# Attention's loads in a fixed order, results through other queues, and projections moved ahead of a diagonal

## The chip, the cores and the metric

The kernel runs on one core of one Trainium2 chip. The metric is the device time of one execution in microseconds (us). Shapes below are partitions x elements, and 2.4 and 1.2 GHz are the two levels of TensorE's clock.

## What is computed

One layer of a streaming encoder on 1024 tokens of width 1024, all in float32: a feed-forward network, a mixer of two head groups, a second feed-forward network, each with a residual and a layer norm. The change touches the mixer alone. Cut to that:

```python
def gla_chunked(q, k, v, log_a):       # 4 heads, dk 64, dv 128, chunks of 64 tokens
    def step(S, inp):
        A = jnp.einsum('bhid,bhjd,bhijd->bhij', qn, kn, jnp.exp(diff))
        o = jnp.einsum('bhij,bhjv->bhiv', A, vn) + jnp.einsum('bhid,bhdv->bhiv', qn * jnp.exp(b), S)
        ...
def dsa_attention(q, k, v, q_idx, k_idx, w_idx):   # 8 heads of 64, blocks of 128 queries
        _, idx = lax.top_k(score, topk)            # 256 keys of each query
        p = jax.nn.softmax(logits, axis=-1)        # over the selected keys
        return jnp.einsum('bqhk,bqkhd->bqhd', p.astype(vg.dtype), vg)

proj = h @ w_in
o_gla = (o.reshape(B, T, GLA_WIDTH) * jax.nn.silu(gg.astype(f32))).astype(h.dtype)
return jnp.concatenate([o_gla, o_dsa], axis=-1) @ w_out
```

## The kernel before

**Products.** A float32 product is made of three passes over a high and a low part (`whi`, `wlo` of the weights, `xh`, `xl` of the input), so one step of a projection is three matmuls (lines 655 to 657 with features on the partitions, tile `pf`; lines 672 to 674 with tokens on the partitions, tile `pt`), and a finished tile takes eight steps, 24 matmuls. Weights come as `raw` tiles of 512 KB (line 71, two buffers of a rotating pool); ACT makes `whi` (line 72), and POOL, in four pieces (line 75), or DVE (line 77) makes `wlo`.

**The stages.** After the first feed-forward network and the index scores come the search for the selected keys (line 785) and the masks (`keep_keys`, lines 820 to 829, on DVE, one call for each block of queries from the third on), which the scheduler spreads over the gated linear attention (GLA). GLA runs as two pairs of heads, `gla_pair(0)` and `gla_pair(1)`. A pair has two halves of 512 tokens. A half starts with a diagonal (line 974 on POOL makes the product `kz`, line 977 on PE sums it to `pd`, line 980 on DVE spreads it into the tile `at`); seven levels follow (POOL line 998, DVE line 999, PE line 1005 to `pa`, DVE line 1016 into `at`), then the products with values and states into `po` (lines 1033 and 1036) and the norm and gate: squares on ACT (line 1044), a root on POOL (line 207), the gate into `og` on DVE (line 1049), and a store to `og_dram` (line 1058). Pair 0 is done when pair 1 begins.

**What fills pair 1.** Pair 1 is a generator, `side`; the generator `fill` gives steps of other projections: first eight token tiles of the pair's own values and gates (`gvg`, lines 672 to 674), then `dq_steps`, eight tiles of attention's queries (lines 655 to 657), four for each half `i` of the tokens. A loop takes one part of `side` and then so many steps of `fill`; PE runs in the order in which this is written, the other engines in an order that a scheduler made. The tuple of counts in that loop has 8 times 8 + 7 times 8 = 120 steps in both kernels. A finished query tile goes through `stage_split`: ACT copies the high part (line 1404), DVE makes the low part (line 1405), and both are stored to DRAM, `q_hi` and `q_lo` (line 1407). Suffix numbers in the names: `q_hi_81` and `q_lo_82` are the first half of the queries, `q_hi_83` and `q_lo_84` the second; `k_hi_85` and `k_lo_86` are the first half of the keys, `k_hi_87` and `k_lo_88` the second.

**Attention** (`attend`) reads all that again in another layout. Keys go into `kst`, two tiles for even and odd heads, here named `xh` and `xl` (line 1545), values into `vt` (line 1546); a block's queries go into a pair `qq`, `ql` (lines 1072 and 1073), of which there are two, filled in turn by `load_q`. For each of eight blocks of 128 queries and each head there are logits (lines 1100 and 1101, tile `lg`), the mask and the maximum on DVE (line 1104), the exponential on ACT (line 1116), transposes (line 1127), and the product with values (line 1143). When a block starts, `begin` loads the GLA result of that block, `cat` (line 1555); `end` turns it (line 194) and, a block later, makes a part of the output projection (lines 672 to 674), for which the weights `raw` of `in_w_out` are wanted.

**Queues.** Every DMA of the kernel before is issued by SP, in one order. An instruction of SP that waits holds back all that stand behind it. A DMA also waits for the one eight places ahead of it, since completion is counted on eight semaphores in rotation.

Of the kernel before, what the change touches and what calls it, by code (L numbers as in the profile page):

```python
# [7 lines left out]
F32 = mybir.dt.float32  # L8
# [10 lines left out]
P = 128  # L19
# [6 lines left out]
HT = T // 2  # L26
# [89 lines left out]
class Block:  # L116
# [759 lines left out]
    def gla_pair(self, p, g, gp, go, sgp, ps, masks, consts, o_dram):  # L876

        nc = self.nc
# [77 lines left out]
        for i in range(2):  # L956
# [7 lines left out]
            for step, L in enumerate((0, 64, 32, 16, 8, 4, 2, 1)):  # L964
# [22 lines left out]
                n = HT // (2 * L)  # L987
# [51 lines left out]
            for h in range(2):  # L1039
# [8 lines left out]
                for j in range(4):  # L1048
# [8 lines left out]
                c0 = p * 256 + h * P  # L1057
                nc.sync.dma_start(
                    o_dram[i * HT : (i + 1) * HT, c0 : c0 + P].rearrange("(b t) f -> t b f", t=P), og
# [125 lines left out]
    def run(self):  # L1185
# [160 lines left out]
        with ExitStack() as s2:  # L1346
# [8 lines left out]
            with ExitStack() as s3:  # L1355
# [45 lines left out]

                def stage_split(pt, dst, t, i):
                    part = [sgp.tile([P, 512], F32R, tag=f"og{j}", name=self.uid("part")) for j in range(2)]
                    nc.scalar.activation(part[0], pt, AF.Copy)
                    nc.vector.tensor_sub(part[1], pt, part[0])
                    for j in range(2):
                        nc.sync.dma_start(dst[i][j][t * P : (t + 1) * P, :], part[j].bitcast(F32))

# [70 lines left out]
                def dq_steps():  # L1479
                    for i in range(2):  # L1480
                        for t, u in enumerate(um["dq"]):
                            for k, pt in enumerate(self.proj_steps(u, i, x1T)):
                                if i == 0 and t < 2 and k == 3:
                                    self.w.need(um["dq"][t + 2], um["dq"][t + 2], 1)
                                if k < KD - 1:
                                    yield
                            stage_split(pt, q_dram, t, i)
                            yield
# [18 lines left out]
                with self.in_order():  # L1507
                    for n in (14,) + (6,) * 7 + (8, 0, 0, 0) + (7,) * 8:
                        next(side)
                        for _ in range(n):  # L1510
                            next(fill)
                    for _ in side:
                        pass
# [17 lines left out]
            for i, pool in enumerate((q0, q1)):  # L1531
# [4 lines left out]
                qp.append((qq, ql))  # L1536
                self.load_q(i, q_dram, qp[i])
            vt = [p.tile([P, 4, 512], F32, name=f"vt{i}") for i, p in enumerate((vp0, vp))]
            def load_keys(i):
                cs = slice(i * HT, (i + 1) * HT)  # L1540
                for e in range(2):
                    for j in range(2):
                        r0 = 64 * (e ^ j)
                        src = k_dram[i][j].rearrange("(q e d) t -> e d q t", e=2, d=64)
                        nc.sync.dma_start(kst[e][r0 : r0 + 64, :, cs].bitcast(F32), src[e])
                nc.sync.dma_start(vt[i], dv_dram[i].rearrange("(b t) f -> t b f", t=P))

            load_keys(0)
            c0 = self.new_half(1)
            cat = []  # L1550
            with tc.tile_pool(name="ps_att", bufs=1, space=PSUM, reuse_waits="tile") as ps:
                def begin(b):
                    c = catp.tile([P, D], F32, tag="cat", name=self.uid("cat"))
                    cat.append(c)
                    nc.sync.dma_start(c[:, 0:512], og_dram[b * P : (b + 1) * P, :])
                    if b == 0:
                        self.w.need(um["out"][0], um["out"][0] + 3)
                    if b == 1:
                        load_keys(1)
                    return c  # L1560
# [11 lines left out]

                self.attend(kst, vt, bias, q_dram, qp, ep, tp, rp, ps, begin, end)

        with ExitStack() as st, ExitStack() as ff_stack:
# [112 lines left out]
```

## Time and profile before

| what | value |
|---|---|
| median of 3 runs | 2039.76 us (2038.33 to 2041.39) |
| the profiled execution | 2041.8 us, span 2040.0 us |
| busy share of the span | PE 96%, DVE 72%, ACT 40%, POOL 29% |
| mean granted TensorE clock | 0.983 |
| DMA | 298.43 MB, mean 146 GB/s over the span |
| pair 1 of GLA | about 985 to 1138 us |
| attention | about 1128 to 1305 us |

All times below are microseconds from the start of the span of the profiled execution. A wait is given with the instruction that waited on the left and the one that released it on the right. A matmul's own duration overlaps with the next one; what counts is the distance between two starts.

### The profile page before, as it was taken

Reading aid. Unit: us, or ns where it says so; the run is one execution under the profiler, and the core shown is the slowest. Engines: PE = TensorE matmul, PEld = TensorE weight load, DVE = VectorE, ACT = ScalarE, POOL = GpSimd, SP = SyncE. Lnnn points to the kernel's source line nnn. Section 1 sums busy time; section 2 is a strip of 40 time slices with the busy share of each in tenths; the row PEclk is TensorE's granted clock in tenths of the full one; section 3 lists DMA queues with packets and bytes.
Section 4 is the critical chain, followed back from the end, with each engine's and each line's share of the span. In section 5 each row is a group of like instructions: output and inputs, shape, how many; then the busy total and the mean of one; then the engine's idle time right before and its main releaser. Section 6 shows DMA issues by size and latency. Waiting matters only on the chain.

```text
span 2040.0 us, 26930 instructions
## 1 busy us (share of the span) xinstructions
PE 1958.7 (96%) x9752; PEld 1608.2 (79%) x9752; DVE 1475.2 (72%) x2330; ACT 823.8 (40%) x1321; POOL 587.6 (29%) x499
## 2 busy tenths in 40 slices
PE   8999999999999999999798699999999999999997
PEld 6888888888888788777576578787888888888886
DVE  5587788785668768899973366566687887876577
ACT  4332332324334345898432355333323323334341
POOL 3345445430001102144333000044454454420001
PEclk9999999999999999998899799999999999999999
DMA  5345445469656322022106631342354454478664
GB/s 175 114 143 188 145 154 179 142 224 320 195 179 200 103 83 84 20 63 73 31 27 177 187 91 37 104 155 82 126 181 145 150 177 149 155 274 273 204 193 151
DMA packets 192708, 298.43 MB, mean 146 GB/s; under 512 B 16304, under 2 KB 98368, under 8 KB 192576
## 3 DMA queue, kind: packets, MB, share of 16 engines
q1 hardware_dynamic: 192576, 296.72, 44.8%
q8 instruction: 76, 1.25, 0.3%
q14 instruction: 56, 0.46, 0.1%
HBM read 205.96 MB, written 90.70 MB: 145 GB/s over the span
## 4 chain that ended last, share of the span: by engine, by line
PE 75%; DVE 11%; DMA 5%; issue 3%; POOL 2%; ACT 2%; SPq 1%; POOLq 0%; DVEq 0%; ACTq 0%
PE pd L491 18%; PE pq L319 12%; PE pq L321 12%; PE pq L320 12%; DVE junk L785 3%; PE pf L655 2%; PE pf L656 2%; PE pf L657 2%; PE pv L1143 2%; PE tpe L1127 2%; PE pt L672 2%; PE pt L673 1%; PE pt L674 1%; PE tp L265 1%; DVE ee L991 1%
## 5 line engine op out<-in xcount | busy, mean ns | idle before, releaser
L97 DVE TENSOR_TENSOR wloq<-rw,whiq 128x512 fp32r<-128x512 f32 (+1 forms) x208 | 213.7, 1030 | 111.0 <-ACT whiq L96 110.2
L97 DVE TENSOR_TENSOR wlod<-rd,whid 128x1024 fp32r<-128x1024 f32 x154 | 186.4, 1220 | 129.0 <-ACT whid L96 128.0
L96 ACT ACTIVATE whid<-rd 128x1024 fp32r<-128x1024 f32 x154 | 160.9, 1059 | 244.4 <-PE pd L491 168.8
L96 ACT ACTIVATE whiq<-rw 128x512 fp32r<-128x512 f32 (+1 forms) x208 | 163.4, 806 | 225.0 <-POOL rw L305 94.0
L491 PE MATMUL pd<-wlod,whid 128*128 128x512 f32 x616 | 239.8, 390 | 0.9 <-DVE wlod L97 0.8
L491 PE MATMUL pd<-whid,wlod 128*128 128x512 f32 x616 | 239.3, 389 | 0.0
L491 PE MATMUL pd<-whid 128*128 128x512 f32 x616 | 235.0, 391 | 0.0
L319 PE MATMUL pq<-b_h,whiq 128*128 128x512 f32 x576 | 228.4, 397 | 2.0 <-ACT b_h L96 2.0
L320 PE MATMUL pq<-b_l,whiq 128*128 128x512 f32 x576 | 225.0, 391 | 1.2 <-DVE b_l L97 1.2
L321 PE MATMUL pq<-b_h,wloq 128*128 128x512 f32 x576 | 224.9, 391 | 0.0
L207 POOL TENSOR_TENSOR rs<-ve,neghalf 128x1 f32<-128x1 f32 x24 | 33.8, 1410 | 619.3 <-DVE ve L225 619.3
L431 ACT ACTIVATE c<-c 128x512 f32<-128x512 f32 x80 | 50.5, 632 | 237.4 <-DVE c L355 135.8
L319 PE MATMUL pq<-xh,whiq 128*128 128x512 f32 x352 | 137.7, 391 | 0.0
L321 PE MATMUL pq<-xh,wloq 128*128 128x512 f32 x352 | 137.0, 389 | 0.0
L320 PE MATMUL pq<-xl,whiq 128*128 128x512 f32 x352 | 136.9, 389 | 0.0
L491 PEld LDWEIGHTS pd<-wlod,whid 128*128 128x128 f32 x616 | 115.7, 188 | 25.5 <-DVE wlod L97 2.1
L491 PEld LDWEIGHTS pd<-whid 128*128 128x128 f32 x616 | 115.5, 188 | 24.7 <-ACT whid L96 1.0
L491 PEld LDWEIGHTS pd<-whid,wlod 128*128 128x128 f32 x616 | 115.6, 188 | 24.1
L672 PE MATMUL pt<-whi,xh 128*128 128x512 f32 x320 | 131.9, 412 | 2.4 <-ACT stage L1475 1.5
L673 PE MATMUL pt<-wlo,xh 128*128 128x512 f32 x320 | 128.0, 401 | 0.0
L674 PE MATMUL pt<-whi,xl 128*128 128x512 f32 x320 | 127.6, 400 | 0.0
L319 PEld LDWEIGHTS pq<-b_h,whiq 128*128 128x128 f32 x576 | 108.5, 188 | 23.7 <-ACT b_h L96 2.7
(265 smaller groups left out, 4476.8 us busy)
## 6 DMA issues: line engine op xcount, KB each, us to landing
rw<-in_ffn_w_gu_dram SPq DMA_DIRECT2D x88, 512.0 KB, 4.2
rd<-h_dram SPq DMA_DIRECT2D x154, 256.0 KB, 3.6
h_dram<-c SPq DMA_DIRECT2D x148, 256.0 KB, 3.0
rt<-in_ffn_w_down_dram SPq DMA_DIRECT2D x44, 512.0 KB, 3.5
t_dram<-rt SPq DMA_DIRECT2D x44, 512.0 KB, 2.9
rd<-t_dram SPq DMA_DIRECT2D x88, 256.0 KB, 3.8
rd<-in_ffn_w_down_dram SPq DMA_DIRECT2D x66, 256.0 KB, 4.2
raw<-in_w_in_dram SPq DMA_DIRECT2D x20, 512.0 KB, 3.8
```

The lines of the kernel that those rows point to most:

```text
L96: self.nc.scalar.activation(hi, src, AF.Copy)
L97: self.nc.vector.tensor_sub(lo, src, hi)
L319: mm(bank, wh[:, k, :], xh[:, k, :], start=(start and k == 0), stop=False)
L320: mm(bank, wh[:, k, :], xl[:, k, :], start=False, stop=False)
L321: mm(bank, wl[:, k, :], xh[:, k, :], start=False, stop=(stop and k == 3))
L431: nc.scalar.activation(t, t, AF.Silu)
L491: nc.tensor.matmul(bank, left, right, start=(i == 0 and n == 0), stop=(i == ng - 1 and n == 2))
L655: nc.tensor.matmul(pt[:m], wh[:, k, :m], xh[:, k, :], start=(k == 0), stop=False)
L672: nc.tensor.matmul(pt, xh[:, k, cols], wh[:, k % 2, :], start=(k == 0), stop=False)
L673: nc.tensor.matmul(pt, xh[:, k, cols], wl[:, k % 2, :], start=False, stop=False)
L674: nc.tensor.matmul(pt, xl[:, k, cols], wh[:, k % 2, :], start=False, stop=(k == KD - 1))
L785: V.tensor_scalar(junk[:, :n], scores[b], thr, None, ALU.is_ge, ALU.add, accum_out=cnt)
```

## The change

Four things change. The loop of pair 1 takes 16 steps of `fill` before the first part of `side`, and later counts are smaller by the same 16 in all. Stores of `og` in pair 1 and stores of the second half's queries are issued by ACT, not SP. The loads of `cat` are issued by POOL. The keys and values are loaded in smaller pieces, blocks 0 and 1, then the queries of block 0, then blocks 2 and 3, then the queries of block 1; the second half comes at block 2 instead of block 1; and from there to the end of attention SP issues in the order in which the code is written, apart from the instructions of `end`.

```diff
--- before.py
+++ after.py
@@ -1055,7 +1055,7 @@
                         ALU.mult,
                     )
                 c0 = p * 256 + h * P
-                nc.sync.dma_start(
+                (nc.scalar if p else nc.sync).dma_start(
                     o_dram[i * HT : (i + 1) * HT, c0 : c0 + P].rearrange("(b t) f -> t b f", t=P), og
                 )
                 yield
@@ -1399,12 +1399,12 @@
                 gqk = s3.enter_context(tc.tile_pool(name="gqk", bufs=1, side="right", reuse_waits="tile"))
                 sgp = s3.enter_context(tc.tile_pool(name="stage", bufs=2, side="right", reuse_waits="tile"))
 
-                def stage_split(pt, dst, t, i):
+                def stage_split(pt, dst, t, i, queue=nc.sync):
                     part = [sgp.tile([P, 512], F32R, tag=f"og{j}", name=self.uid("part")) for j in range(2)]
                     nc.scalar.activation(part[0], pt, AF.Copy)
                     nc.vector.tensor_sub(part[1], pt, part[0])
                     for j in range(2):
-                        nc.sync.dma_start(dst[i][j][t * P : (t + 1) * P, :], part[j].bitcast(F32))
+                        queue.dma_start(dst[i][j][t * P : (t + 1) * P, :], part[j].bitcast(F32))
 
                 def dk_items():
                     for t, u in enumerate(um["dk"]):
@@ -1484,7 +1484,7 @@
                                     self.w.need(um["dq"][t + 2], um["dq"][t + 2], 1)
                                 if k < KD - 1:
                                     yield
-                            stage_split(pt, q_dram, t, i)
+                            stage_split(pt, q_dram, t, i, nc.scalar if i else nc.sync)
                             yield
 
                 def gla(p):
@@ -1505,7 +1505,9 @@
 
                 fill = fill()
                 with self.in_order():
-                    for n in (14,) + (6,) * 7 + (8, 0, 0, 0) + (7,) * 8:
+                    for _ in range(16):
+                        next(fill)
+                    for n in (4,) + (6,) * 7 + (4, 0, 0, 0) + (6,) + (7,) * 6 + (6,):
                         next(side)
                         for _ in range(n):
                             next(fill)
@@ -1534,29 +1536,35 @@
                 for e in range(2):
                     nc.gpsimd.memset(ql[64 - e * 64 : 128 - e * 64, e, :, :].bitcast(F32), 0.0)
                 qp.append((qq, ql))
-                self.load_q(i, q_dram, qp[i])
             vt = [p.tile([P, 4, 512], F32, name=f"vt{i}") for i, p in enumerate((vp0, vp))]
-            def load_keys(i):
-                cs = slice(i * HT, (i + 1) * HT)
+
+            def load_keys(b0, b1):
+
+                i, c0, c1 = b0 // 4, b0 % 4 * P, (b1 - 1) % 4 * P + P
                 for e in range(2):
                     for j in range(2):
                         r0 = 64 * (e ^ j)
-                        src = k_dram[i][j].rearrange("(q e d) t -> e d q t", e=2, d=64)
-                        nc.sync.dma_start(kst[e][r0 : r0 + 64, :, cs].bitcast(F32), src[e])
-                nc.sync.dma_start(vt[i], dv_dram[i].rearrange("(b t) f -> t b f", t=P))
-
-            load_keys(0)
+                        src = k_dram[i][j][:, c0:c1].rearrange("(q e d) t -> e d q t", e=2, d=64)
+                        nc.sync.dma_start(kst[e][r0 : r0 + 64, :, b0 * P : b1 * P].bitcast(F32), src[e])
+                rows = dv_dram[i][c0:c1, :]
+                nc.sync.dma_start(vt[i][:, b0 % 4 : (b1 - 1) % 4 + 1, :], rows.rearrange("(b t) f -> t b f", t=P))
+
+            loads = ExitStack()
+            loads.enter_context(self.in_order(mybir.EngineType.SP))
+            for i in range(2):
+                load_keys(2 * i, 2 * i + 2)
+                self.load_q(i, q_dram, qp[i])
             c0 = self.new_half(1)
             cat = []
             with tc.tile_pool(name="ps_att", bufs=1, space=PSUM, reuse_waits="tile") as ps:
                 def begin(b):
                     c = catp.tile([P, D], F32, tag="cat", name=self.uid("cat"))
                     cat.append(c)
-                    nc.sync.dma_start(c[:, 0:512], og_dram[b * P : (b + 1) * P, :])
+                    nc.gpsimd.dma_start(c[:, 0:512], og_dram[b * P : (b + 1) * P, :])
                     if b == 0:
                         self.w.need(um["out"][0], um["out"][0] + 3)
-                    if b == 1:
-                        load_keys(1)
+                    if b == 2:
+                        load_keys(4, 8)
                     return c
 
                 def end(b, c):
@@ -1571,6 +1579,7 @@
                         nc.sync.dma_start(half, xh)
 
                 self.attend(kst, vt, bias, q_dram, qp, ep, tp, rp, ps, begin, end)
+                loads.close()
 
         with ExitStack() as st, ExitStack() as ff_stack:
             xp = st.enter_context(tc.tile_pool(name="sums2", bufs=1, reuse_waits="tile"))
```

On PE, at pair 1's diagonal, the kernel before has:

```order
L886 MATMUL pz_7730<-mT,wa_5343 128x512
L977 MATMUL pd_7909<-heads,kz_6648 128x2 x4
L672 MATMUL pt_7915<-whi_7753,xh_3620 128x512
L673 MATMUL pt_7915<-wlo_7754,xh_3620 128x512
L674 MATMUL pt_7915<-whi_7753,xl_3621 128x512
```

and the changed kernel, after two whole token tiles of 24 matmuls each that stand behind the same `L886`, has:

```order
L672 MATMUL pt_7932<-whi_7783,xh_3620 128x512
L673 MATMUL pt_7932<-wlo_7784,xh_3620 128x512
L674 MATMUL pt_7932<-whi_7783,xl_3621 128x512
L977 MATMUL pd_7963<-heads,kz_6648 128x2 x4
L672 MATMUL pt_7969<-whi_7753,xh_3620 128x512
```

So 48 matmuls have moved from behind the diagonal `pd` to ahead of it.

On SP, ahead of attention, the kernel before ends its key loads (`k_hi_87`, `k_lo_88` being the keys of the second half) with:

```order
L1545 DMA xh_9560<-k_hi_87 64x4x512
L1545 DMA xh_9560<-k_lo_88 64x4x512
L1545 DMA xl_9561<-k_hi_87 64x4x512
L1546 DMA vt_9578<-dv_dram_89 128x4x512
L1545 DMA xl_9561<-k_lo_88 64x4x512
L1407 DMA q_hi_83<-part_8625 128x512
L1407 DMA q_lo_84<-part_8626 128x512
L1072 DMA qq_9562<-q_hi_81 64x8x128
L1073 DMA ql_9563<-q_lo_82 64x4x128
```

and the changed kernel begins its loads with:

```order
L1548 DMA xh_9560<-k_hi_85 64x4x256
L1548 DMA xh_9560<-k_lo_86 64x4x256
L1407 DMA q_hi_81<-part_8567 128x512
L1407 DMA q_lo_82<-part_8568 128x512
L1548 DMA xl_9561<-k_hi_85 64x4x256
L1548 DMA xl_9561<-k_lo_86 64x4x256
L1550 DMA vt_9570<-dv_dram_89 128x2x512
L1072 DMA qq_9562<-q_hi_81 64x8x128
L1073 DMA ql_9563<-q_lo_82 64x4x128
```

Two more loads of `qq_9562` and `ql_9563` follow in both. The queries of block 0 now stand behind the keys of two blocks, not of eight, and stores of the second half's queries (`q_hi_83`) are no longer there. The four loads of `qq_9566` and `ql_9567` (block 1) come after five loads for blocks 2 and 3, and six `raw` of `in_w_out` after those.

On POOL, at the end of pair 1 (`grs` is the root of the norm, `wlo` a low part of a weight of the output projection), the kernel before has:

```order
L75 TENSOR_TENSOR wlo_9640<-raw_9638,whi_9639 128x256 x4
L1535 MEMSET ql_9563 64x512 x2
L75 TENSOR_TENSOR wlo_9649<-raw_9647,whi_9648 128x256 x4
L207 TENSOR_TENSOR grs_8768<-ss_8760,neghalf 128x4
L207 TENSOR_TENSOR grs_8783<-ss_8775,neghalf 128x4
L1535 MEMSET ql_9571 64x512 x2
```

and the changed kernel, after the same two roots and the clearing of `ql`, has:

```order
L75 TENSOR_TENSOR wlo_9627<-raw_9625,whi_9626 128x256 x4
L75 TENSOR_TENSOR wlo_9636<-raw_9634,whi_9635 128x256 x4
L1563 DMA cat_9623<-og_dram 128x512
L1563 DMA cat_9809<-og_dram 128x512
L1563 DMA cat_9995<-og_dram 128x512
L1563 DMA cat_10202<-og_dram 128x512
L75 TENSOR_TENSOR wlo_9645<-raw_9643,whi_9644 128x256 x4
L75 TENSOR_TENSOR wlo_9654<-raw_9652,whi_9653 128x256 x4
```

The low parts of four weights, which stood ahead of the roots or between the levels, now stand behind them, with four loads of `cat` in their middle. On PE, the last query tile (24 matmuls of `pf`, written over the PSUM of one of pair 1's last `po`) stands ahead of the first logits in the changed kernel; before, four heads' logits stood ahead of it.

## Rows read from the trace of the kernel before

**Rows 1.** Windows: length; busy us (count) PE, PEld, DVE, ACT, POOL; PEclk; DMA share; GB/s

```profile
985.00:1055.00 70.00, 53.83 (x313) 42.64 (x312) 68.71 (x124) 26.75 (x49) 21.43 (x18) 0.87 0.07 20
1055.00:1117.38 62.38, 59.87 (x356) 48.82 (x356) 24.07 (x47) 23.41 (x46) 27.85 (x35) 0.96 0.54 139
1117.38:1179.31 61.93, 40.08 (x231) 30.83 (x229) 22.54 (x88) 19.50 (x69) 3.05 (x4) 0.81 0.70 191
1179.31:1300.00 120.69, 117.19 (x1048) 96.42 (x1050) 80.68 (x200) 66.33 (x136) 0.00 (x0) 1.00 0.19 47
```

**Rows 2.** Waits of PE, 975 to 1180: line, awaited; us in total, times, longest

```profile
PE pd L977 <- POOL kz L974: 13.2, 1, 13.2
PE lg L1100 <- DMA qq<-q_hi: 10.1, 1, 10.1
PE tp L194 <- DMA cat<-og_dram: 7.3, 1, 7.3
PE po L1033 <- DVE at L1016: 3.0, 1, 3.0
```

**Rows 3.** Timeline of PE round pair 1's diagonal: start, duration, instruction [idle before, releaser]

```profile
999.07 1.87 PE L977 MATMUL pd<-heads,kz 128*128 128x2 f32 x8 [13.19 <-POOL kz L974]
...
1002.65 0.63 PE L673 MATMUL pt<-wlo,xh 128*128 128x512 f32 x1
1003.08 0.63 PE L674 MATMUL pt<-whi,xl 128*128 128x512 f32 x1
...
1009.07 0.39 PE L674 MATMUL pt<-whi,xl 128*128 128x512 f32 x1
1009.30 0.39 PE L672 MATMUL pt<-whi,xh 128*128 128x512 f32 x1
```

**Rows 4.** Timeline of POOL: the diagonal's product and four pieces of one weight

```profile
997.18 1.84 POOL L974 TENSOR_TENSOR kz<-gk,gq 128x512 f32<-128x512 f32 x1 [5.03 <-DVE bT L902]
...
1104.27 2.80 POOL L75 TENSOR_TENSOR wlo<-raw,whi 128x256 fp32r<-128x256 f32 x4 [3.54 <-ACT whi L72]
```

**Rows 5.** Timeline of DVE at the end of pair 1's first half

```profile
1048.10 0.75 DVE L826 TENSOR_SCALAR keep<-score,search 128x1024 f16<-128x1024 f32 x1
...
1049.30 0.73 DVE L827 TENSOR_TENSOR keep<-keep 128x1024 f16<-128x1024 f16 x1
...
1051.38 0.41 DVE L829 TENSOR_SCALAR score<-keep 128x1024 bf16<-128x1024 f16 x1
...
1053.54 1.29 DVE L1016 COPY_PREDICATED at<-mask,pa 128x256 f32<-128x256 uint8 x2
```

**Rows 6.** Timeline of SP: first key load, query loads of block 0, GLA results

```profile
1095.98 0.67 SPq L1545 DMA_DIRECT2D xl<-k_hi  x1
...
1110.30 0.92 SPq L1072 DMA_DIRECT2D qq<-q_hi  x1
...
1151.26 10.24 SPq L1555 DMA_DIRECT2D cat<-og_dram  x5
```

**Rows 7.** DMA, 1090 to 1165: all traffic; issues: count, KB each, median us to landing

```profile
DMA packets 12885, 15.80 MB, mean 211 GB/s; under 512 B 720, under 2 KB 6864, under 8 KB 12880
...
qq<-q_hi SPq DMA_DIRECT2D x6, 256.0 KB, 7.8
raw<-in_w_out_dram SPq DMA_DIRECT2D x3, 512.0 KB, 7.7
```

**Rows 8.** Waits of SP's queue, 1090 to 1165

```profile
SPq L1555 <- DMA q_lo<-part: 4.9, 1, 4.9
```

**Rows 9.** Timeline of PE: last products of pair 1, the projection after them, the turning of `cat`

```profile
1133.21 0.61 PE L1036 MATMUL po<-state,qe 128*128 128x128 f32 x4
...
1137.94 0.50 PE L655 MATMUL pf<-xh,whi 128*128 128x512 f32 x1 [1.74 <-DVE og L1049]
...
1144.90 0.40 PE L657 MATMUL pf<-xh,wlo 128*128 128x512 f32 x1
...
1160.06 1.09 PE L194 MATMUL tp<-ident,cat 128*128 128x128 f32 x4 [7.29 <-DMA cat<-og_dram]
```

## The prediction on record

> **What bounds the kernel now.** I read the windows first, for the four stages round the change [rows 1]. Before 985 and after 1179 TensorE (PE) has little to give: from 1179 to 1300 it is busy 117.19 of 120.69 us at full clock. Between them lie 194 us in which it is not: 53.83 of 70.00 busy, at a mean clock of 0.87, in the first half of GLA's pair 1; 59.87 of 62.38 in its second half; and 40.08 of 61.93, at 0.81, where GLA ends and attention begins. Idle time is thus 16.2, 2.5 and 21.9 us. In the first of these windows VectorE (DVE) is busy 68.71 of 70.00: PE waits there, but DVE is the bound. The list of PE's waits then gives four names that hold most of the idle time [rows 2]: the diagonal of pair 1 (13.2, released by POOL), a block's queries (10.1, a DMA), the GLA result `cat` (7.3, a DMA), and the products of the first half (3.0, DVE). Last, PE's timeline shows what a long wait costs behind it [rows 3]: after the diagonal's 13.19 us, matmuls start 0.43 us apart (1002.65, 1003.08), the lower of the two clock levels, and later 0.23 apart (1009.07, 1009.30).
>
> **Part 1, 48 matmuls ahead of the diagonal.** They take 48 x 0.23 = 11 us at full clock and begin when PE now goes idle, at 999.07 - 13.19 = 985.9. The diagonal is released by POOL's line 974, which runs from 997.18 to 999.02, itself held by DVE [rows 4]; that doesn't move. So the 11 us fit, and about 2 us of idle time stay. If PE ran them at the low level they would take 48 x 0.43 = 20.6 and hold the diagonal up by 7.5; PE is at full clock just before, so I count that in the range only. But what those 11 us free is not gained at once. The fill steps behind the diagonal are fewer, PE arrives earlier at the products of the first half, and those wait for DVE, which has no idle time to give. DVE's own work ahead of its last step of that half (line 1016) shrinks only by what the new order puts behind it, the last mask's lines 826, 827 and 829: 0.75 + 0.73 + 0.41 = 1.9 us [rows 5]. So the first half ends about 2 us sooner. By then PE has done 62 fill steps where it had done 56 (16 + 4 + 7 x 6 against 14 + 7 x 6); six steps of three matmuls, 18 x 0.23 = 4.1 us, are gone from the second half, where PE is the bound (59.87 of 62.38). **Gain of part 1: 2 + 4 = 6 us.** Bounds: 0, if DVE or a late tile takes it all; and 21, if PE alone were the bound (16.2 + 2.5 idle and some 2 of low clock).
>
> **Parts 2 to 4, queues and order.** Now the keys of all eight blocks (4 MB) and 1 MB of values go out from 1095.98 on, and the queries of block 0 only from 1110.30 [rows 6]; issued one behind another they land by 1127.84, where PE has waited 10.1. In the changed order only the keys of two blocks (1 MB) and half the values stand ahead. The queries' issue is then set by PE's last state update, which stands ahead of 1117.38, the end of the second window, less the 6 us: at the latest 1111, and with 7.8 us to land [rows 7] 1119. PE's first logits come 15.6 us behind that end (worked out below), at 1127. That wait goes: **10.1**. `cat`: its five loads took 10.24 us to issue [rows 6], of which 4.9 was a wait on SP for a query store that had to land [rows 8]. From another queue that wait is not in front of it: **7.3**, if nothing else is late (below). The low clock behind each of the two: 24 matmuls of `pf` ran from 1137.94 to 1144.90 + 0.23 = 7.2 us [rows 9], against 24 x 0.23 = 5.5; 1.7 for such a stretch, **3.4** for two.
>
> A new wait comes in. The last query tile stands ahead of the first logits, and it needs the PSUM of pair 1's last products, so squares, root and gate lie bare. Now the last products start at 1133.21 and end some 0.35 later (four starts 0.1 apart), and the tile starts at 1137.94, 4.4 later, of which logits hid all but 1.74 [rows 9]: **minus 2.7**. The gate's results and twelve query and result stores are issued by ACT. No row shows a DMA issued by ACT; SP's issues of these sizes take 0.67 to 0.92 [rows 6], and ACT is busy 19.5 of 61.9 [rows 1], so I take nothing, with 6 x 0.7 = 4 us as the bound if six stand ahead of the squares.
>
> The weights of the output projection are what is late next. The low parts of four were made ahead of attention; now all six `raw` stand behind the queries of block 1, which wait for pair 1's last product. From PE's last fill step before those products (1117.38 now; X): products to X + 4, `raw` issued at X + 6, landing after 5 to 7.7 (512 KB, [rows 7]), one ACT copy, then 2.80 on POOL for each [rows 4]: two low parts by X + 19 to X + 21. Then four `cat` loads. No row shows a DMA issued by POOL: 0.7 (SP's) to 2.8 (POOL's longest piece of work here), I take 1 each, near SP's, as the engine only issues. `cat` of block 0 lands about X + 24 to X + 27. PE wants it after 4 (products), 4.4 (chain), 7.2 (tile), 11 (block 0: the rest of it ran from 1145.1 to 1160.06 - 7.3 = 1152.8 [rows 9], 7.6, and I take 3.4 for the four heads that came earlier): X + 26.6. A stall of 0 to 4: **minus 2**. Third and fourth low parts: X + 21 + 4 + 5.6 = X + 31 at most, wanted some 9 us behind `cat`, X + 36; no stall.
>
> **Gain of parts 2 to 4: 10.1 + 7.3 + 3.4 - 2.7 - 2 = 16 us.** Bounds: 0 with the rival below, 21 with no stall and the chain hidden. After block 1 the work is the same and PE is the bound at full clock; the keys of blocks 4 to 7, now asked for at block 2, have 17 us and more until block 4. I count nothing there.
>
> **The sum.** 2041.8 - 6 - 16 = 2019.8 for the profiled execution, which is 2 above the median of 2039.76; against the median 2017.8, so 2018.
>
> **Rivals.**
> A. *DVE takes part 1 whole.* The first half ends where it did, and later waits on DVE eat the six steps. For it: DVE at 98% there. Against: in the second half DVE is busy 24.07 of 62.38. Time: 2040 - 16 = 2024.
> B. *PE bound throughout pair 1.* If the scheduler's masks give way to the levels, part 1 brings 12 to 21: 2003 to 2012. Against it: the order on DVE moves only 1.9 us of work.
> C. *POOL's loads are slow, somewhat.* With c us for each of four loads, the fourth weight is ready at X + 27 + 4c and PE wants it at X + 36; the queries of block 2 are issued behind it. The stall is 4c - 9, in place of the 2 in the sum: with c of 4 to 6 it is 7 to 15, and the time 2023 to 2031.
> D. *The same, and slower than before.* 4c - 9 must exceed 24 (the gain without a stall) and 4 more, so from c = 9.3 on: 2044 and more. It is one mechanism: POOL, the two low parts behind its four loads, PE's first output projection, and SP's queries of block 2. Against it: POOL's longest piece here is 2.8 [rows 4], and DVE, which could hold it off, is busy in 22.54 of 61.93 [rows 1]. The Trainium skill ("SBUF — State Buffer", SBUF: two separate sides) warns of it: a DMA issued by GpSimd has its descriptors written by that engine, and some DVE operations lock it out meanwhile. No run here shows a DMA on that queue.
> E. *`cat` is late from any queue.* 15.80 MB move between 1090 and 1165 at 211 GB/s [rows 7]; a load that shares with them can land as late as before. Then 7.3 and one low stretch of 1.7 stay, without the 2 for the weights: 2018 + 7 = 2025. Against it: of the 10.24 us, 4.9 was a wait in the queue [rows 8], and six 512 KB weights are all that moves then. The Trainium skill ("DMA: Bandwidth & Descriptors", Rules for kernel authors) speaks for E: spreading DMAs over issuing engines doesn't help bandwidth and saves only issue time. The trace shows such an issue time only as that queue's wait.
> F. *The loads do not do what they say.* The queries of block 0 land no sooner, since the stores from ACT take the same DMA engines, and the weights' wait replaces that for `cat`: parts 2 to 4 bring 0 to 2, and part 1 is lost as in A: 2038 to 2040.
>
> **How the numbers follow.** Forecast (2009 to 2023) 0.53; A (2023 to 2026) 0.13; B 0.09; C 0.10; D 0.05; E 0.04; F 0.06. The range leaves out D, F and the far end of B: 2005 to 2034 holds about 0.87. 0.2% is 4 us, about what a measurement of this kernel can tell from no change. Faster by over 0.2%: the forecast, A, B, C and E, 0.89; within: F, 0.06; slower: D, 0.05.
>
> **What would show it.** In the changed profile: the wait of `pd` down from 13.2 to about 2, no low clock behind it; the first half's `po` still waiting for DVE, for longer than 3.0; no wait of `lg` on `qq`; a wait of 4 to 5 of `pf` on `og`; a wait of `tp` on `cat`, or of `pt` on `wlo`, of 0 to 4 in all; 1179.31 to come at about 1157. The prediction is wrong if `pt` or `tp` waits over 8 us on POOL or on a POOL load, if `pd` comes later than 1003, or if PE waits anew in blocks 2 to 5 for queries or keys.

## The result, and the profile after

| | before | changed |
|---|---|---|
| median | 2039.56 us (4 runs, 2038.33 to 2041.39) | 2022.68 us (4 runs, 2021.52 to 2023.18) |
| ratio | | 0.9916, 95% interval 0.9899 to 0.9933 |
| profiled execution: span, clock | 2040.0, 0.983 | 2020.7, 0.990 |

The change gains 16.9 us; 22 were forecast, the range reached from 2005 to 2034. For the first three stages of [rows 1], the windows of the changed kernel are (length; busy us and count of PE, PEld, DVE, ACT, POOL; clock; DMA share; GB/s):

```profile
985.00:1055.00 70.00, 61.17 (x349) 47.70 (x347) 69.02 (x130) 31.66 (x60) 25.41 (x21) 0.98 0.06 16
1055.00:1115.00 60.00, 57.94 (x362) 48.06 (x363) 29.36 (x54) 18.56 (x40) 16.18 (x18) 0.97 0.50 140
1115.00:1179.00 64.00, 52.21 (x342) 39.16 (x341) 33.95 (x121) 31.61 (x94) 17.59 (x26) 0.95 0.89 223
```

In the first stage PE is busy 61.17 of 70 (53.83 before) at a clock of 0.98 (0.87 before, 0.92 in the repeat below), and DVE still 69.02: DVE is the bound there as it was. Where GLA ends and attention begins, PE is busy 52.21 of 64, with 223 GB/s of DMA. PE's waits between 985 and 1290, which answer to [rows 2]:

```profile
PE po L1033 <- DVE at L1016: 5.3, 1, 5.3
PE pf L655 <- DVE og L1049: 4.4, 1, 4.4
PE pkv L943 <- ACT mT L933: 3.2, 1, 3.2
PE lg L1100 <- DMA qq<-q_hi: 1.9, 1, 1.9
PE pv L1143 <- DVE et L1132: 1.6, 1, 1.6
```

The diagonal's 13.2, the queries' 10.1 and the 7.3 for `cat` are gone from the top of the list. The first half's `po` waits 5.3 for DVE instead of 3.0, the last query tile `pf` waits 4.4 for the gate `og`, as forecast. One name is new where none was expected: `lg` waits again for queries, 1.9. That is not block 0 but block 3. PE's timeline there (start, duration, instruction, idle before):

```profile
1169.82 0.47 PE L1100 MATMUL lg<-xh,qq 128*128 128x512 f32 x1 [1.86 <-DMA qq<-q_hi]
...
1172.15 1.55 PE L1143 MATMUL pv<-et,vt 128*64 128x128 f32 x12 [1.63 <-DVE et L1132]
```

After the first logits of block 3 (128x512) had come late, the next product waited 1.63 more, and the matmuls behind run at the lower clock (the 12 small ones of the last line take 1.55; the same group took 0.88 at 1165.93). SP's timeline says why those queries came late:

```profile
1118.73 23.23 SPq L71 DMA_DIRECT2D raw<-in_w_out_dram  x6
1142.01 0.58 SPq L1072 DMA_DIRECT2D qq<-q_hi  x1
...
1144.64 0.62 SPq L1548 DMA_DIRECT2D xh<-k_hi  x1
...
1150.33 0.60 SPq L1550 DMA_DIRECT2D vt<-dv_dram  x1
1151.03 0.57 SPq L1072 DMA_DIRECT2D qq<-q_hi  x1
1151.65 3.04 SPq L1073 DMA_DIRECT2D ql<-q_lo  x1
...
1155.54 6.10 SPq L1073 DMA_DIRECT2D ql<-q_lo  x1
```

The six weights take SP from 1118.73 to 1141.96, since each `raw` after the second waits for a low part on POOL to free its buffer (POOL's fourth ends at 1141.56, and the last `raw` goes out at 1141.59). Then come the queries of block 2 (1142.01), five loads of the second half's keys and values (2 MB and 1 MB, 1144.64 to 1150.93, the last issue's end), and only then those of block 3, whose last issue ends at 1161.64. Two of these four issues took 3.04 and 6.10 us of SP, where block 2's took about 0.6: behind 3 MB of loads the queries not only stand later, their issue itself is slower. What makes it slower is not shown. They land at 1169.8, and PE wanted them at 1169.82 - 1.86 = 1168.0.

**Where the time went.** The diagonal came 3.5 us later here than before (1002.57 against 999.07), with the same program up to there. A repeat (below) has it at 999.49, so that is a difference between executions, and the repeat is the better one to set beside before. Stage by stage:

| mark on PE | before | changed, repeat | gain so far |
|---|---|---|---|
| diagonal of pair 1 starts | 999.07 | 999.49 | -0.4 |
| products of the first half | 1054.31 | 1052.82 | 1.5 |
| second half's diagonal | 1065.89 | 1061.30 | 4.6 |
| last fill step ends (X) | 1117.38 | 1108.81 | 8.6 |
| `cat` of block 0 is turned | 1160.06 | 1135.83 | 24.2 |
| `cat` of block 1 | 1178.46 | 1153.69 | 24.8 |
| `cat` of block 2 | 1196.83 | 1178.40 | 18.4 |
| span | 2040.0 | 2020.9 | 19.1 |

The gain reaches 24.8 us and 6.3 of them are given back inside block 2. Rows of that table for before (those that are not shown above) and for the repeat:

```profile
1054.31 2.22 PE L1033 MATMUL po<-gv,at 128*128 128x128 f32 x8 [2.98 <-DVE at L1016]
...
1178.46 0.66 PE L194 MATMUL tp<-ident,cat 128*128 128x128 f32 x4
...
1196.83 0.66 PE L194 MATMUL tp<-ident,cat 128*128 128x128 f32 x4
```

```profile
999.49 1.48 PE L977 MATMUL pd<-heads,kz 128*128 128x2 f32 x8 [1.92 <-POOL kz L974]
...
1052.82 2.23 PE L1033 MATMUL po<-gv,at 128*128 128x128 f32 x8 [6.15 <-DVE at L1016]
...
1108.81 0.38 PE L1033 MATMUL po<-gv,at 128*128 128x128 f32 x2
...
1135.83 0.66 PE L194 MATMUL tp<-ident,cat 128*128 128x128 f32 x4
...
1149.21 0.41 PE L1100 MATMUL lg<-xh,qq 128*128 128x384 f32 x1 [1.47 <-DMA qq<-q_hi]
...
1153.69 0.66 PE L194 MATMUL tp<-ident,cat 128*128 128x128 f32 x4
...
1178.40 0.66 PE L194 MATMUL tp<-ident,cat 128*128 128x128 f32 x4
```

Block 2 takes 18.4 us before and 24.7 in the repeat, with the same work. The queries of block 2 (the row with 128x384) are late there too, by 1.47, which lies in block 1.

### The profile page after: what moved, and what is told of

The parts are those of the page before. It is cut to its first block, busy times and chain, and to the rows that moved or that the text cites. A ratio compares the mean times of both kernels' runs of the same rounds, so it can differ in the third digit from the quotient of the medians.

```text
span 2020.7 us, 26955 instructions
## 1 busy us (share of the span) xinstructions
PE 1956.5 (97%) x9752; PEld 1606.6 (80%) x9752; DVE 1482.4 (73%) x2330; ACT 824.0 (41%) x1321; POOL 592.1 (29%) x507
## 4 chain that ended last, share of the span: by engine, by line
PE 77%; DVE 11%; DMA 4%; ACT 3%; issue 3%; POOL 2%; SPq 0%; POOLq 0%; DVEq 0%; ACTq 0%
PE pd L491 18%; PE pq L320 13%; PE pq L319 13%; PE pq L321 13%; DVE junk L785 3%; PE pf L655 3%; PE pf L656 3%; PE pf L657 3%; PE pv L1143 2%; PE tpe L1127 1%; PE pt L672 1%; PE pt L674 1%; PE pt L673 1%; DMA rd<-in_ffn_w_down_dram 1%; PE tp L265 1%
## 5 line engine op out<-in xcount | busy, mean ns | idle before, releaser
L491 PEld LDWEIGHTS pd<-whid,wlod 128*128 128x128 f32 x616 | 115.6, 188 | 24.2
L321 PEld LDWEIGHTS pq<-b_h,wloq 128*128 128x128 f32 x576 | 108.7, 189 | 23.1
```

The lines of the kernel that those rows point to most:

```text
L321: mm(bank, wl[:, k, :], xh[:, k, :], start=False, stop=(stop and k == 3))
L491: nc.tensor.matmul(bank, left, right, start=(i == 0 and n == 0), stop=(i == ng - 1 and n == 2))
```

## The experiments

All times are medians; each ratio is to the kernel before on the same chip.

**The changed kernel again.** 

> The changed kernel as it is, once more. Theory: that its diagonal of pair 1 came 3.5 us later than before's (1002.57 against 999.07) although the program up to there is the same is a difference between two executions; here the diagonal comes anywhere from 998 to 1003, and the time is 2020 to 2024. Rival: the change makes what stands ahead of the diagonal late; then the diagonal is again at 1002 or later and the time 2022 to 2023.

Measured: 2022.05 us, 0.9910 (0.9896 to 0.9924). The diagonal came at 999.49. The 3.5 us were no effect of the change. And they show something else: the repeat was 2.1 us earlier at X (1108.81 against 1110.88), 0.9 earlier at the turning of block 1's `cat` (1153.69 against 1154.59), and not earlier behind block 2.

**Part 1 undone.**

```diff
-                    for _ in range(16):
-                        next(fill)
-                    for n in (4,) + (6,) * 7 + (4, 0, 0, 0) + (6,) + (7,) * 6 + (6,):
+                    for n in (14,) + (6,) * 7 + (8, 0, 0, 0) + (7,) * 8:
```

> The changed kernel with the old counts of fill steps (part 1 undone). Theory: part 1 is worth 6 us, 2 where DVE bounds the first half and 4 behind it; time 2028 to 2030, with PE's wait at the diagonal back at 13 and no wait at line 1005 or 1016 over 3. Rival A (DVE takes it whole): 2022 to 2024. Rival B (PE is the bound in all of pair 1): 2034 or more.

Measured: 2027.17 us, 0.9935 (0.9921 to 0.9948), so part 1 is worth 5.1 us in the median, a little under the 6 to 8 expected, and neither rival's figure. The wait at the diagonal is 13.2 again. In the trace X comes at 1114.61, 5.8 later than in the repeat, and `cat` of block 0 at 1141.73, 5.9 later.

**Part 1 alone**, the same edit the other way round on the kernel before.

> The kernel before with part 1 alone (48 matmuls ahead of the diagonal). Theory: part 1 is worth the same 5 to 6 here, and attention's two waits (queries 10, cat 7) stay: time 2034 to 2036. Rival A: the DMAs set the pace at attention's start, so that PE only arrives earlier and waits longer for the queries: 2038 to 2041.

Measured: 2037.33 us, 0.9985 (0.9977 to 0.9994), 11 runs from 2033.92 to 2041.22. That is 1 to 5 us, between the two expectations. In the profiled execution (2034.69, among the shorter ones) X comes at 1110.82, 6.6 sooner than before, but PE waits longer for the first queries (the row's last part is the idle time ahead of it):

```profile
1122.65 0.55 PE L1100 MATMUL lg<-xh,qq 128*128 128x256 f32 x1 [11.45 <-DMA ql<-q_lo]
```

11.45 where it was 10.08: 1.4 of what part 1 saves is taken by the transfers at attention's start. In this execution 1.0 comes back at `cat` (a wait of 6.3 instead of 7.3), and the whole span is 7.4 shorter than before's, so the waits don't explain why the median gains only 1 to 5. The times of this kernel scatter over 7 us, those of before in the same series over 5; why was not found.

**The second half's keys behind the queries of block 3.**

```diff
-                    if b == 2:
+                    if b == 3:
                         load_keys(4, 8)
```

> The second half's keys and values are asked for at block 3 instead of block 2, so behind the queries of block 3. Theory: the 5 us that block 2 loses against before (1154.59 to 1177.91 between two turnings of cat, 23.3, against 18.4) come from those queries lying behind 3 MB of keys; the wait of lg on qq (1.9), the one of pv behind it (1.6) and the low clock go, time 2017 to 2019. Rival: the DMA engines are simply full there, and the keys, now later, make block 4 wait for them; time 2021 to 2024 with a wait of lg on a key load at about 1195.

Measured: 2015.97 us, 0.9885 (0.9871 to 0.9899), and in a second series 2017.99, 0.9894 (0.9877 to 0.9910). SP now issues the queries of block 3 ahead of the keys, and block 2 takes 18.4 us, as before the change:

```profile
1145.95 0.58 SPq L1072 DMA_DIRECT2D qq<-q_hi  x1
...
1148.61 0.62 SPq L1548 DMA_DIRECT2D xh<-k_hi  x1
```

```profile
1152.05 0.66 PE L194 MATMUL tp<-ident,cat 128*128 128x128 f32 x4
...
1170.41 0.66 PE L194 MATMUL tp<-ident,cat 128*128 128x128 f32 x4
```

The first fence is SP (the first load of the queries, then the first of the keys), the second PE. No wait on a key load comes in its place. So the loss in block 2 is the order of these loads, and not the number of bytes. The size of the gain is less sure than the place: of the eight executions in both series five took 2015.5 to 2016.2 us and three 2020.2 to 2020.8. Both profiles are of the five; what costs the three some 5 us more was not traced.

**`cat` on SP again**, in the fixed order.

```diff
-                    nc.gpsimd.dma_start(c[:, 0:512], og_dram[b * P : (b + 1) * P, :])
+                    nc.sync.dma_start(c[:, 0:512], og_dram[b * P : (b + 1) * P, :])
```

> The changed kernel with cat loaded through SP again, in the fixed order, so block 0's cat stands between the queries of block 1 and the six weights of the output projection. Theory (what matters is what waits in front in the queue): SP waits there until the GLA results have landed, about 1126 (issued by ACT at 1120.4, 5.6 to land), where the weights were issued from 1118.7; the first output projection and block 2's queries come 5 to 10 later; time 2026 to 2033. Rival (the issuing queue only saves issue time): 2021 to 2024.

Measured: 2029.33 us, 0.9947 (0.9933 to 0.9960), 7.3 slower than the repeat. The time is the theory's, but the place was another. SP and PE:

```profile
1120.50 0.34 SPq L1563 DMA_DIRECT2D cat<-og_dram  x1
1121.37 29.27 SPq L71 DMA_DIRECT2D raw<-in_w_out_dram  x6
...
1151.26 0.58 SPq L1072 DMA_DIRECT2D qq<-q_hi  x1
```

```profile
1158.24 0.66 PE L1100 MATMUL lg<-xh,qq 128*128 128x384 f32 x1 [7.21 <-DMA qq<-q_hi]
```

SP waits for the results until 1120.50, so the weights go out from 1121.37 (1116.66 in the repeat) and end at 1150.64 (1141.41). The output projection of block 0 hardly notices: three waits of 0.2 to 0.4 on `wlo`. It is block 2's queries behind the weights that are late: `lg` waits 7.21. `cat` itself is hardly later (block 0's is turned at 1136.9, without a wait). And the queue is not alone in this: the weights start 4.7 later and end 9.2 later. The scheduler put ACT's copies of them (line 72) elsewhere as well: the first comes at 1135.53, behind exponentials of block 0, where in the repeat it comes at 1123.97, ahead of them. How much of the 7.3 is the wait in the queue and how much ACT's new order was not separated.

**The stores on SP again** (part 2 undone: `nc.sync` in lines 1058 and 1407).

> The changed kernel with the stores of late queries and of pair 1's results on SP again (part 2 undone). Theory: the stores of the results wait for the gate and stand on SP ahead of the weights, which are issued 2 to 5 later; 0 to 4 us lost, time 2022 to 2027. Rival: ACT's twelve issues (0.33 to 0.75 each in the changed kernel's trace) lengthen the chain from squares to gate, and without them it is faster, under 2021.

Measured: 2026.47 us, 0.9933 (0.9918 to 0.9948), 4.4 slower than the repeat; the theory's side. (The rival's 0.75 is half of a row that merges two issues and the gap between them; an issue by ACT took 0.33 to 0.40 there.) SP and PE:

```profile
1117.64 1.50 SPq L1058 DMA_DIRECT2D og_dram<-og  x2
...
1121.88 1.12 SPq L71 DMA_DIRECT2D raw<-in_w_out_dram  x2
```

```profile
1130.61 0.48 PE L1127 MATMUL tpe<-ident,e 128*128 128x128 f32 x1 [4.46 <-ACT e L1116]
```

```profile
1127.34 1.06 ACT L72 ACTIVATE whi<-raw 128x1024 fp32r<-128x1024 f32 x1 [11.06 <-DMA raw<-in_w_out_dram]
...
1130.08 0.39 ACT L1116 ACTIVATE e<-e,nm 128x128 f32<-128x128 f32 x1
```

SP waits for the gate until 1117.64, the weights start at 1121.88. What PE feels is not the weights but an exponential (second fence, PE; third, ACT): ACT's copies of them (line 72) stand ahead of the exponentials of block 0 in ACT's order, and the first of them waited 11.06 for its load; the first exponential comes at 1130.08, and `tpe` waits 4.46 on ACT. So the theory had the cause, not the path by which it reaches PE.

**More fill in the first half.**

```diff
-                    for n in (4,) + (6,) * 7 + (4, 0, 0, 0) + (6,) + (7,) * 6 + (6,):
+                    for n in (4,) + (7,) * 7 + (4, 0, 0, 0) + (5,) + (6,) * 7:
```

> Seven more fill steps in the first half of pair 1 (7 instead of 6 behind each level), seven fewer in its second. Theory: DVE sets the end of the first half (its last line 1016 ended 1056.0), PE waited 5.3 us there, and seven steps of 0.68 us fill that wait: the first product still starts at 1055 to 1057, the wait is under 1, and the second half is 4.8 shorter; time 2017 to 2019. Rival: PE's steps delay what DVE waits for, the product starts 3 to 5 later and nothing is gained; time 2021 to 2024.

Measured: 2020.53 us, 0.9902 (0.9889 to 0.9916): 1.5 gained where 4.8 were expected, no more than the two intervals leave open, and PE still waits 5.0. The theory failed. DVE at the end of that half, in the repeat and here:

```profile
1052.05 1.30 DVE L1016 COPY_PREDICATED at<-mask,pa 128x256 f32<-128x256 uint8 x2
...
1054.03 1.21 DVE L826 TENSOR_SCALAR keep<-score,search 128x1024 f16<-128x1024 f32 x1
```

```profile
1052.13 0.74 DVE L826 TENSOR_SCALAR keep<-score,search 128x1024 f16<-128x1024 f32 x1
...
1053.91 0.41 DVE L829 TENSOR_SCALAR score<-keep 128x1024 bf16<-128x1024 f16 x1
1054.51 1.29 DVE L1016 COPY_PREDICATED at<-mask,pa 128x256 f32<-128x256 uint8 x2
```

In the repeat the last line 1016 stands ahead of the mask's lines 826, 827 and 829; with the other counts the scheduler put those three ahead of it again, and the half ended 2.5 later (1055.28 against 1052.82 for the first product). The counts moved DVE's order, so this run could not tell whether PE has any part in the bound.

**A short mask for the last block.** In `keep_keys`, for that block alone:

```diff
+        if b == NB - 1:
+            cum = big().bitcast(F16)[:, :n]
+            V.tensor_scalar(cum, score, tau, None, ALU.is_ge)
+            bias = score.bitcast(BF16)[:, :n]
+            V.tensor_scalar(bias, cum, -1.0, -DROP, ALU.add, ALU.mult)
+            return bias
```

> The changed kernel with a short mask for the last block of queries: two operations on DVE (the scores against the threshold, and the bias) where there were some ten; the exact count among equal scores and the next higher threshold are left out for that block. About 9 us less DVE work in pair 1's first half. Theory (DVE sets the end of that half): PE's wait of 5 to 6 at its first product falls to 0 to 2 and the half ends 4 to 6 earlier; at the end of attention's block 1 that is still there, though block 3's queries may hold some of it up in block 2; first turning of cat 4 to 6 earlier. Rival: PE or the chain over POOL and ACT sets it; the half ends within 1 us of where it did.

Measured: 2014.00 us, 0.9873 (0.9859 to 0.9886). The first product comes without a wait (its line is 1039 in this kernel):

```profile
1048.44 1.05 PE L1039 MATMUL po<-gv,at 128*128 128x128 f32 x8
```

1048.44 against 1052.82, although this execution's diagonal was at 1000.41. The wait of 6.15 is gone and `cat` of block 0 comes at 1128.39, 7.4 earlier. DVE does set the end of the first half.

**The whole mask, behind the first half.** Nothing is left out; each DVE instruction of the last block's mask is ordered behind the last line 1016 of that half:

```diff
+                        if p and not i:
+                            self.half_end = self.nc.cur_bb.bb.instructions[-1].name
...
+        if b == NB - 1:
...
+                if ins.engine == mybir.EngineType.DVE:
+                    self.tc.add_manual_dep(
+                        ins,
+                        self.half_end,
+                        mybir.DependencyInfo(mybir.DependencyClass.NoSync, mybir.DependencyReason.DATA),
+                        reason="in_order",
+                    )
```

> The changed kernel with nothing left out, but the whole mask of the last block of queries ordered on DVE behind the last line 1016 of pair 1's first half. Theory (DVE sets that half's end; in the second half it is busy half of the time): PE's wait at the first product, 5 to 6, goes, the half ends 5 to 6 earlier, and the turning of block 0's cat, 1135.83 in the repeat of the changed kernel, comes at 1130 to 1132; of that, block 3's queries hold back some in block 2, as with the short mask; time 2015 to 2018. Rival: the mask's ten operations now hold up DVE in the second half by as much as they freed in the first: cat at 1134 or later, time 2020 to 2023.

> Both: the second half's keys asked for at block 3, and the last mask behind pair 1's first half. Theory: the two gains add, as they lie in different places (6 in block 2, 5 to 6 in pair 1): 2009 to 2012. Rival: what comes earlier out of pair 1 waits for the weights and queries, whose chain over POOL and SP doesn't start earlier by as much: 2013 to 2016.

Measured: 2021.51 us, 0.9909 (0.9892 to 0.9925) with the mask alone; 2017.25 us, 0.9886 (0.9871 to 0.9901) with the later keys as well, no better than those by themselves. (The first of the two also has `b == 2` for `b == 3` in a condition of the second layer norm's loop. That lies behind 1300 and leaves the stages compared as they are, but its total is not that of the mask alone.) Of the first expectation the rival was right: block 0's `cat` comes at 1135.0, against 1135.8 in the repeat. Of the second neither was: what was gained in the first half did not come out of pair 1 at all. The half ends earlier and the second half gives it back. PE with both edits:

```profile
1047.72 1.05 PE L1048 MATMUL po<-gv,at 128*128 128x128 f32 x8
...
1063.40 1.12 PE L1018 MATMUL pa<-qz,kz 64*64 64x64 f32 x16 [4.65 <-DVE ss L1060]
```

The product comes at 1047.72, but DVE then works on the mask, and for 3.6 on the gates, until 1063, where it is wanted for the second half's start and the first half's gate, and PE waits 4.65 at the first level (line 1018 here is line 1005 of before). The last fill step ends at 1107.15; with the keys alone it was 1107.06.

**The mask where DVE has room.** The same dependency, on the first line 1016 of the second half.

```diff
-                        if p and not i:
+                        if p and i and L == 32:
```

> The second half's keys at block 3, and the last mask ordered on DVE behind the first level with line 1016 of pair 1's second half, where the levels leave DVE idle, instead of behind the first half's end. Theory (a late start of the second half took the gain back: DVE carried the mask from 1048 to 1058 while PE waited 4.7 us for the gate's sums): that wait goes, the last products start at 1101 to 1104 (1107.1 with the mask where it was or behind the half), time 2010 to 2013. Rival: the mask costs its 9 us wherever it lies in pair 1, last products at 1106 to 1108, time 2015 to 2018.

> The changed kernel with the second half's keys at block 3 once more, to stand beside the mask's new place on the same chip. Both theories: 2015 to 2017, block 2 takes 18.4 us between two turnings of cat, last products at 1106 to 1109.

Measured: **2008.24 us, 0.9843 (0.9828 to 0.9857)** with both edits, beside 2017.99 with the keys alone in the same series, and less than the 2010 to 2013 expected. It beats the changed kernel by some 14 us. The profiled executions of the two differ by 7.8 (spans of 2006.1 and 2013.9). Windows of it, the first stage and then up to its X:

```profile
985.00:1055.00 70.00, 67.00 (x389) 53.72 (x388) 59.03 (x113) 33.65 (x63) 27.46 (x27) 0.95 0.06 16
1055.00:1101.00 46.00, 45.86 (x289) 36.90 (x288) 33.12 (x62) 13.57 (x31) 10.05 (x11) 1.00 0.54 158
```

PE is busy 67.00 of 70 in the first stage and 45.86 of 46 after; DVE falls to 59.03 there and rises to 33.12 of 46 behind it. X is at 1100.90, with the keys alone at 1107.06 and 1108.1.

## Why the prediction was right, and where it was not

**Part 1: 6 forecast, 5 to 6 measured in the changed kernel.** 5.1 in the median with part 1 undone, 5.8 to 5.9 in the traces; on the kernel before, part 1 alone brought 1 to 5 in the median. The steps held: the diagonal's wait fell from 13.2 to 1.9 (repeat), the first half's product came 1.5 sooner where 1.9 was read from the masks' rows [rows 5], and DVE bounds that half, which the short mask shows. The clause on rival A, that it takes part 1 whole, is refuted; rival B too. One sign failed, "no low clock behind it". In the repeat, after 1.92 us without a matmul, the granted clock was 0.50, the lower level, from 1000 to 1006, with matmuls 0.43 apart:

```profile
1002.68 0.63 PE L673 MATMUL pt<-wlo,xh 128*128 128x512 f32 x1
1003.11 0.63 PE L674 MATMUL pt<-whi,xl 128*128 128x512 f32 x1
```

Twelve matmuls cost 12 x 0.2 = 2.4 us there. In the changed kernel's first profile the wait was 0.77 and the clock stayed at 1.00, and with the short mask it stayed at 1.00 after 2.20. The half can have lost little by it, as PE still had 6.15 to spare at its end.

**What was gained and not forecast in pair 1.** X came 8.6 sooner in the repeat, 6 were in the sum. The 2.5 us wait of `pf` on line 1405 is gone. It is still there, 2.2, with part 1 alone, and it is gone in all runs that have the new order of loads, with the stores on either queue. In its place `po` waits 1.2 on the same line, behind X. What in the new order takes the first away was not tried; that four weights are no longer split on ACT and POOL just there is the likeliest reason, and only argued.

**Parts 2 to 4 up to block 1: 16 forecast, 16.2 measured.** From X to the turning of block 1's `cat` it is 61.1 us before and 44.9 in the repeat. PE's windows for the two:

```profile
1117.38:1178.46 61.08, 39.42 (x227) 30.41 (x226) 21.85 (x87) 19.34 (x68) 3.05 (x4) 0.80 0.70 191
1108.81:1153.69 44.88, 35.41 (x228) 27.08 (x226) 22.25 (x87) 23.24 (x72) 17.50 (x25) 0.92 0.81 214
```

PE is idle 9.5 instead of 21.7, so 12.2 less, where the terms without the clock make 12.7; it is busy 4.0 less for the same matmuls, at 0.92 instead of 0.80, where the clock's term was 3.4. Of the terms, the queries' 10.1 and `cat`'s 7.3 went, and the chain of squares, root and gate lies bare for 4.4 exactly as worked out. The stall of 2 at `cat` or the weights did not come; 1.2 of `po` and 1.5 of `lg` on block 2's queries, which stand on SP behind the weights, came instead, and that these make about as much is luck. No run undoes the order of the loads alone. That it is what takes away the queries' 10.1 follows from the rest: with part 1 alone the wait stays (11.45), and it is gone with `cat` or with the stores back on SP.

POOL's timeline in the changed kernel, the two low parts, the four loads, the next two:

```profile
1125.07 5.57 POOL L75 TENSOR_TENSOR wlo<-raw,whi 128x256 fp32r<-128x256 f32 x8 [3.58 <-ACT whi L72]
1130.57 0.74 POOL L1563 DMA_DIRECT2D cat<-og_dram  x1
1134.36 1.63 POOL L1563 DMA_DIRECT2D cat<-og_dram  x3 [3.05 <-DVE nm L1115]
1136.01 5.55 POOL L75 TENSOR_TENSOR wlo<-raw,whi 128x256 fp32r<-128x256 f32 x8
```

The four loads took 1130.57 to 1135.99, 1.4 each instead of 1; 0.55 to 0.74 is the issue, and 3.05 is one pause, at whose end the second load is released by DVE, as after 1.91 in the repeat and 2.70 with the later keys. The profile has it as an ordinary wait; of the lock that the Trainium skill ("SBUF — State Buffer", SBUF: two separate sides) warns of no row here shows a sign, and none rules it out. At `cat` it cost nothing, as a load landed in 4.6 (median) and PE turned the first at 1137.4 without a wait. But the third and fourth low parts stand behind the four loads, and with them the last two `raw` and all that SP issues after those, to X + 31 (1141.56) as the prediction has it. Rivals C and D needed 4 and 9.3 for each load, and fall. So does E, as `tp` does not wait for `cat` at all, and F, with the time itself.

The Trainium skill ("DMA: Bandwidth & Descriptors", Rules for kernel authors) says that spreading DMAs over engines saves only issue time; as to bandwidth no run disagrees (211 GB/s before, 223 in the changed kernel's window), but a queue that stands still for a result holds back all behind it: with the stores back on SP the first weights went out 5.2 later (1121.88 against 1116.66). The two stores ahead of them took 1.5 of that to issue, the rest is SP's wait for the gate, and the time was 4.4 longer. The measurement decides.

**The step that failed: "I count nothing there".** The keys of blocks 4 to 7 were looked at as something that block 4 needs, 17 us later, and so it is. What they stand in front of on SP was not priced: the queries of block 3, behind 3 MB. That cost 5.0 us in the profiled execution and 6.3 in the repeat, and moving them one block down gives 4 to 6 us back. The prediction had named the sign itself, PE waiting anew for queries in blocks 2 to 5, and it came: 1.86 in block 2's end for block 3 in the profiled execution, 1.47 and 2.13 in the repeat. The sum 22 - 6.3 + 2.6 = 18.3 is near what the traces show (19.1), the medians 16.9; the profiled execution of before was 2 above its median. That the 2.6 not forecast in pair 1 covered a part of this loss is luck.

**A pinned mark.** With block 3's queries late, time saved ahead of block 2 is partly not saved: the repeat's 2 us at X were gone at the end, because the queries wait for the weights, and their chain over ACT and POOL did not come earlier: the first `raw` went out 2.1 sooner (1116.66 against 1118.73), but POOL's first low part started at 1125.16 against 1125.07, and the last `raw` was out at 1141.41 against 1141.96. The prediction added its gains as if each reached the end.

## What to carry to other kernels

When loads are put in a fixed order, price for each load what stands behind it in the queue, not only when its own data are wanted; a large early load is paid by the small one that follows. Work put into an engine's idle time is worth no more than the next engine allows: read the busy share of the others in that window, and look where the work that bounds it could go. It pays to move it into a stretch where its engine is half idle, and not just past the point where it hurts: the same mask, moved by a few places, gained nothing, and moved a little further, 8 to 10 us.

## What the runs showed of the hardware

In the changed kernel a DMA issued by POOL took 0.55 to 0.74 us of that engine, and one by ACT 0.33 to 0.40; most of SP's took 0.3 to 0.7, but behind 3 MB of loads two took 3.04 and 6.10. `cat` landed in 4.6 by POOL and in 4.0 by SP before (medians of six and five loads). After 1.92 us without a matmul TensorE's granted clock was 0.50 in the repeat, and 1.00 after 2.20 in the kernel with the short mask. Two executions of one program differed by 3.1 us at the diagonal of pair 1 (1002.57 and 999.49) and by 0.2 at the end.
